# Hybrid attention layer on one core: other fillers in the head, and loads, a bias matmul and weight splits of the head in other places

## The chip, the cores and the metric

The kernel runs on one core of one Trainium2 chip. The time is device microseconds of one execution; three executions of the kernel before gave 317.7, 318.25 and 319.02 us, and 318.25 is their median.

## The reference, cut to what matters

One decoder layer for 512 tokens of width 1024. The head of the kernel, which the change touches, computes the modulation, the norm, and the first projection:

```
mod = silu(c) @ w_ada + b_ada
shift, scale, gate = jnp.split(mod, 3, axis=-1)
h = rms_norm(x, norm_gain) * (1 + scale[:, None, :]) + shift[:, None, :]
proj = h @ w_in
...
return x + gate[:, None, :] * out
```

`proj` splits into queries, keys, values and gates of two groups of heads (a sliding window of 128 with sinks; compressed, selected and window branches), whose outputs are gated, put together, multiplied by `w_out` and added to x. The relative bias of the heads comes from a table of 32 buckets.

## The kernel before, in words

x is held transposed, as eight tiles `xT[k]` of 128 features by 512 tokens. One block of the code, under `in_order`, fixes the order of every engine's instructions to that in which they are written; it holds all of the head and the first projection (about the first 54 us). What comes after is written through generators, and a scheduler places it on the engines.

**Norm.** ScalarE (ACT) squares each `xT[k]` as it lands, VectorE (DVE) adds the squares of four tiles into one accumulator (`sq` for tiles 0 to 3, `sacc` for 4 to 7; tile 7 in two halves), and TensorE (PE) sums each accumulator over the partitions into `pr` (L330). DVE makes the reciprocal root `rx` of the four blocks of tokens in some nine small steps; PE transposes it into `rbp`, a row of factors on all partitions (L352); ACT keeps a copy, `rb` (L364). `scaled(k)` multiplies `xT[k]` by it (DVE, L270).

**Modulation.** Each tile k needs a shift and a scale per feature, in `AB[:, k]`. For k = 0 and 1 PE computes them: `mod_pe(k)` multiplies silu(c) in `scz` by eight column blocks of w_ada in `ada[k]` (L230), ACT copies the result to `macc` (L233), `mod_col(k)` sums it over the partitions on PE (L250), and `mod_ab(k)` writes AB on DVE (L255, L256). For k = 2 to 7 DVE does it alone: `mod_rows(k)` is two long multiply-and-sum instructions (L222) over `ada[k]` and `scrow`, the row silu(c) on all partitions. scrow is made from the row c that a DMA broadcasts: ACT computes `throw` (L373), DVE multiplies (L376).

**First projection.** For each k, `h_high` makes hh[k] and hf[k] on ACT (L276; L363, L365 for k = 0), `h_low` their difference hl[k] on DVE (L279); the weights `wst[k]` are split by ACT into swh (`weights_high`, L262) and by DVE into swl (`weights_low`, L265). `first_proj(k, n)` is eight matmuls (L286, L287): n = 0 takes hh and swh, n = 1 hh and swl, n = 2 hl and swh. Between n = 1 and n = 2 of tile k stands `new_tile(k + 1)`, that is h_high(k+1), mod_rows(k+2), h_low(k+1), scaled(k+2) and the split of weights k+2. In what follows FP is the start of first_proj(0, 0), and T the start of mod_rows(2).

**Loads.** All go through SyncE's queue (SP): eight tiles of x, `first` (c as a column, b_ada, the gain, the identity), `bl` (the table for the relative bias), then ada[k] and wst[k] by turns, the row c after wst[0], and `rest`. ada_ring and wst_ring hold four tiles each. ada[k] comes in two halves.

**Fillers.** `dummies(n)` are n matmuls of a zero tile of 512 columns (L312), whose results nobody reads. The table ND says how many stand at five places: 20 at the start, 4 after the first sums, 2 after the bias matmul and before mod_pe(0), 2 between the transposes and mod_col(0), 3 after it.

**Relative bias.** PE multiplies the two parts of `bl` (L343) into `pl`, ACT copies the result to `lsb` (L345) and spreads its last columns (L346), and two DMAs write it to `line_d`, from where the attention reads it at about 49 us.

Of the kernel before, what the change touches and what calls it, by code (L numbers as in the profile page):

```python
# [13 lines left out]
AF = mybir.ActivationFunctionType  # L14
OP = mybir.AluOpType
# [4 lines left out]
S, D, HD, NB = 512, 1024, 64, 4  # L20
# [5 lines left out]
LINE = 640  # L26
# [3 lines left out]
WAIT_L, WAIT_M = 4, (0, 8)  # L30
PER_A, PER_B = 3.6, (3.5, 1.6, 7)
NEAR = 256
ND = (20, 2, 2, 3, 4)
NR = 4
LW = 4
PE_MODS = 2
# [45 lines left out]
def hybrid_layer_kernel(ctx, tc, A, out):  # L82
# [117 lines left out]
    def load_ada(k):  # L200
        t = ada_ring[:, k % NR]
        if k < PE_MODS:
            ada[k] = t.rearrange("p (a b c) -> p a b c", a=8, b=2)
            for e in range(2):
                SP.dma_start(ada[k][:, 4 * e:4 * e + 4], A["w_ada_cols"][k][:, 4 * e:4 * e + 4])
        else:
            ada[k] = t.rearrange("p (a b) -> p a b", a=2)
            for e in range(2):
                SP.dma_start(ada[k][:, e], A["w_ada_rows"][k - PE_MODS][:, e])

    def load_wst(k):
        wst[k] = wst_ring[:, k % NR]
        SP.dma_start(wst[k], A["w_qkv_a"][k])
# [8 lines left out]
            DVE.tensor_tensor_reduce(out=ada[k][:, e], in0=ada[k][:, e], in1=scrow, scale=factor, scalar=start,  # L222
                                     op0=OP.mult, op1=OP.add, accum_out=AB[:, k, 1 - e:2 - e])

    def mod_pe(k):

        pm = ps_pj.tile([128, 512], F32, name="pj")[:, 0:256]
        for j in range(8):
            c = j % 4
            PE.matmul(pm[32 * c:32 * c + 32, :], scz[:, j, :], ada[k][:, j].rearrange("p a b -> p (a b)"),  # L230
                      start=j < 4, stop=j >= 4, skip_group_check=True)
        macc[k] = stp.tile([128, 2, 128], F32, name="macc0", bufs=2)
        ACT.activation(macc[k].rearrange("p a b -> p (a b)"), pm, AF.Copy)  # L233
# [18 lines left out]
    def mod_ab(k):  # L252

        pc = pcs.pop(k)
        DVE.tensor_tensor(AB[:, k, 1:2], pc[:, 0:1], prm[:, k:k + 1], op=OP.add)  # L255
        DVE.scalar_tensor_tensor(AB[:, k, 0:1], pc[:, 1:2], prm1[:, k:k + 1], prm[:, 24 + k:25 + k],  # L256
                                 op0=OP.add, op1=OP.mult)

    def weights_high(k):

        ws[k] = (stp.tile([128, 768], F32R, name="swh", bufs=3), stp.tile([128, 768], F32R, name="swl", bufs=3))
        ACT.activation(ws[k][0], wst[k], AF.Copy)  # L262

    def weights_low(k):
        DVE.tensor_tensor(ws[k][1], wst[k], ws[k][0].bitcast(F32), op=OP.subtract)  # L265
# [24 lines left out]
    with in_order(tc) as begun:  # L290
        zero = con.tile([128, 512], BF16, name="zero")
        DVE.memset(zero, 0.0)
        DVE.memset(ada_ring[:, 0, 0:1], 0.0)
        DVE.memset(wst_ring[:, 0, 0:1], 0.0)
        POOL.memset(lsb[0:8, 0:LINE - NEAR], BIG)
        for k in range(8):
            SP.dma_start(xT[k], A["xT"][k])
        SP.dma_start(first, A["first"])
        SP.dma_start(bl, A["bias"])
        for k in range(NR):  # L300
            load_ada(k)
            load_wst(k)
            if k == 0:
                src = A["c"]
                SP.dma_start(scrow, bass.AP(tensor=src.tensor, offset=src.offset, ap=[[0, 128], [1, D]]))
        SP.dma_start(rest, A["rest"])
        DVE.memset(scz, 0.0)


        def dummies(n):  # L310
            for _ in range(n):
                PE.matmul(pj_kv[0].rearrange("p a b -> p (a b)"), zero[:, 0:128], zero, start=True, stop=True)  # L312

        dummies(ND[0])

        halves = [slice(0, 256), slice(256, 512)]
        pr = ps_pj.tile([128, 512], F32, name="pj")
        pl = pj_q[1][0:40, 0:NEAR]
        th = con.tile([128, 8], F32, name="th")
        for k in range(8):  # L320
            sq = stp.tile([128, S], F32, name="sacc") if k == 4 else T2(F32, "sq")
            if k % 4 == 0:
                sacc = sq
            for c in (halves if k == 7 else [slice(0, S)]):
                ACT.activation(sq[:, c], xT[k][:, c], AF.Square)
                if k % 4:
                    DVE.tensor_tensor(sacc[:, c], sacc[:, c], sq[:, c], op=OP.add)
            if k % 4 == 3:
                for tb in range(NB):
                    PE.matmul(pr[:, tb:tb + 1], sacc[:, tb * 128:(tb + 1) * 128], ones, start=k == 3 and tb == 0,  # L330
                              stop=k == 7 and tb == NB - 1, skip_group_check=True)
            if k == 3:
                dummies(ND[4])
        ACT.activation(th, cT, AF.Tanh, scale=0.5)
        DVE.scalar_tensor_tensor(sc_col, th, 1.0, cT, op0=OP.add, op1=OP.mult)
        DVE.tensor_scalar(scz[:, :, 0], sc_col, 0.5, None, op0=OP.mult)
        sx = con.tile([128, NB], F32, name="sx")
        DVE.tensor_scalar(sx, pr[:, 0:NB], 1.0 / D, EPS, op0=OP.mult, op1=OP.add)
        rx = rsqrt(sx, NB)
        DVE.tensor_scalar(prm1, prm[:, 8:16], 1.0, None, op0=OP.add)  # L340
        DVE.tensor_tensor(prmg[:, 0:8], prm1, prm[:, 24:32], op=OP.mult)
        DVE.tensor_scalar(prmg[:, 8:16], prm[:, 24:32], 0.5, None, op0=OP.mult)
        PE.matmul(pl, bl[:, NEAR:NEAR + 40], bl[:, 0:NEAR], start=True, stop=True)  # L343
        dummies(ND[1])
        ACT.copy(lsb[0:40, LINE - NEAR:LINE], pl)  # L345
        ACT.copy(lsb[32:40, 0:LINE - NEAR], lsb[32:40, LINE - NEAR:LINE - NEAR + 1].to_broadcast([8, LINE - NEAR]))  # L346
        for a in range(2):
            SP.dma_start(line_d[a], lsb[32 * a:32 * a + 8, :])
        mod_pe(0)
        rbp = ps_pj.tile([128, 512], F32, name="pj")  # L350
        for tb in range(NB):
            PE.transpose(rbp[:, tb * 128:(tb + 1) * 128], rx[:, tb:tb + 1].to_broadcast([128, 128]), ident)  # L352
        dummies(ND[2])
        mod_col(0)
        dummies(ND[3])
        weights_high(0)
        scaled(0, rbp, halves[:1])
        mod_ab(0)
        scaled(0, rbp, halves[1:])
        rb = stp.tile([128, S], F32, name="rb")  # L360
        hf[0] = T2(F32, "hf")
        for c in halves:
            ACT.activation(hh[0][:, c], y[0][:, c], AF.Identity, bias=AB[:, 0, 1:2], scale=AB[:, 0, 0:1])  # L363
        ACT.activation(rb, rbp, AF.Copy)  # L364
        ACT.activation(hf[0], y[0], AF.Identity, bias=AB[:, 0, 1:2], scale=AB[:, 0, 0:1])  # L365
        weights_low(0)
        scaled(1, rb)
        h_low(0)
        weights_high(1)
        weights_low(1)  # L370
        throw = T2(F32, "throw"), T2(F32, "throw")
        for e in range(2):
            ACT.activation(throw[e], scrow[:, 512 * e:512 * e + 512], AF.Tanh, scale=0.5)  # L373
        for e in range(2):
            v = scrow[:, 512 * e:512 * e + 512]
            DVE.scalar_tensor_tensor(v, throw[e], 1.0, v, op0=OP.add, op1=OP.mult)  # L376

        def new_tile(k):

            h_high(k, halves if k < 4 else (slice(0, S),))  # L380
            if k < 7:
                mod_rows(k + 1)
            h_low(k)
            if k < 7:
                scaled(k + 1, rb)
                weights_high(k + 1)
                weights_low(k + 1)

        for k in range(8):
            if k + NR < 8:  # L390
                load_ada(k + NR)
                load_wst(k + NR)
            elif k == LW:
                for _ in range(5):
                    load_next()
            for n in range(3):
                first_proj(k, n)
                if k == 0 and n == 0:
                    mod_pe(1)
                if k < 7 and n == 1:  # L400
                    if k == 0:
                        mod_col(1)
                        mod_ab(1)
                    new_tile(k + 1)
                if k >= 6 and n == 1:
                    split_to("kv_cmp", 2 * (k - 6) + 1, 0)
        DVE.tensor_tensor(kg[:, 0], qga, kga, op=OP.mult)
        DVE.tensor_tensor(kg[:, 1], qgb, kgs, op=OP.mult)
        DVE.tensor_tensor(kg[:, 2], qgb, kgw, op=OP.mult)
        DVE.tensor_tensor(kg[:, 3], qgb, kgc, op=OP.mult)  # L410
        DVE.tensor_scalar(kg[:, 0:3], kg[:, 0:3], -(HD ** -0.5), None, op0=OP.mult)
        DVE.tensor_scalar(kg[:, 3], kg[:, 3], HD ** -0.5, None, op0=OP.mult)
        DVE.tensor_scalar(nsink, sinks, -1.0, None, op0=OP.mult)
# [678 lines left out]
```

## Time and profile before

| what | value |
|---|---|
| median of three executions | 318.25 us |
| the profiled execution | 317.4 us, of which the profile's span is 315.6 us |
| PE / DVE / ACT busy | 307.2 / 237.4 / 195.7 us |
| first_proj(0, 0) begins (FP) | 17.63 us |
| mod_rows(2) begins on DVE (T) | 22.46 us |
| the first projection ends, the next matmuls begin | 54.34 us |

The profiled execution lies 0.85 us below the median of the three others. All clock times below are microseconds from the start of its span. A row of the timeline has the start, the length, the engine with the line of the code, the operation with what it writes and reads, and the count of instructions merged into it.

### The profile page before, as it was taken

What the parts mean: (1) busy time and instruction counts of PE and PEld (TensorE: products, weight loads), DVE (VectorE), ACT (ScalarE), POOL (GpSimd) and SP (SyncE); (2) the same over time, 40 slices, a digit from 0 to 9 for tenths busy, and PEclk for the clock granted to TensorE, in tenths of its full rate; (3) what the DMA queues carried; (4) which work ended last, traced back from release to release, by engine and by line L of the source; (5) the groups of instructions that cost most, each with busy time, mean ns of one, the idle gap of its engine ahead of it and who ended that gap; (6) DMA issues with size and microseconds to landing.
All of it is one profiled execution on the core that took longest, in us unless ns stands there. A gap on an engine that the chain in (4) does not pass through costs nothing.

```text
span 315.6 us, 5830 instructions
## 1 busy us (share of the span) xinstructions
PE 307.2 (97%) x2122; PEld 252.3 (80%) x2122; DVE 237.4 (75%) x658; ACT 195.7 (62%) x472; POOL 3.9 (1%) x21
## 2 busy tenths in 40 slices
PE   8899999999999999999999999999999999999995
PEld 3468888788988999889883888878788878788885
DVE  3589999999967558898997998988686777544221
ACT  5476557668967675676927767778785777513000
POOL 0000000000000000000000000000000000000000
PEclk9799999999999999999999999999999999999999
DMA  7999967900291908170553004222320210242201
GB/s 241 380 412 411 405 233 197 340 11 0 62 345 35 293 5 251 51 266 2 175 177 145 5 2 133 69 66 70 134 69 0 69 66 3 74 159 98 104 33 69
DMA packets 28232, 44.65 MB, mean 141 GB/s; under 512 B 1787, under 2 KB 19612, under 8 KB 28204
## 3 DMA queue, kind: packets, MB, share of 16 engines
q1 hardware_dynamic: 27052, 42.18, 39.4%
q10 hardware_dynamic: 1152, 2.10, 2.0%
q8 instruction: 17, 0.28, 0.4%
q14 instruction: 11, 0.09, 0.1%
HBM read 42.13 MB, written 2.14 MB: 140 GB/s over the span
## 4 chain that ended last, share of the span: by engine, by line
PE 79%; DVE 10%; ACT 6%; DMA 2%; issue 1%; SPq 1%; POOL 0%; ACTq 0%; DVEq 0%; POOLq 0%
PE pj L469 29%; PE pj L459 9%; PE sq L286 8%; PE po L930 7%; PE s L855 7%; PE pt L913 4%; PE skv L287 4%; PE pt L903 3%; PE s L588 3%; DVE qs L520 2%; DMA xTp<-in_xT 2%; DVE kTb L538 1%; PE po L936 1%; DVE raw L690 1%; DVE wl L174 1%
## 5 line engine op out<-in xcount | busy, mean ns | idle before, releaser
L173 ACT ACTIVATE wh<-raw 128x512 fp32r<-128x512 f32 (+1 forms) x52 | 31.2, 637 | 13.5 <-PE pj L469 13.4
L174 DVE TENSOR_TENSOR wl<-raw,wh 128x512 fp32r<-128x512 f32 (+1 forms) x52 | 34.8, 689 | 5.2 <-ACT wh L173 3.5
L459 PE MATMUL pj<-wh,hh 128*128 128x256 f32 (+1 forms) x128 | 37.0, 289 | 0.0
L459 PE MATMUL pj<-wl,hh 128*128 128x256 f32 (+1 forms) x128 | 36.7, 287 | 0.1
L459 PE MATMUL pj<-wh,hl 128*128 128x256 f32 (+1 forms) x128 | 36.6, 286 | 0.0
L867 ACT ACTIVATE pp<-pp,nm 128x256 f32<-128x256 f32 (+2 forms) x48 | 29.3, 614 | 6.6 <-DVE nm L860 6.4
L469 PE MATMUL pj<-hh,wh 128*128 128x512 f32 x80 | 32.1, 402 | 0.0
L469 PE MATMUL pj<-hh,wl 128*128 128x512 f32 x80 | 32.0, 400 | 0.0
L469 PE MATMUL pj<-hl,wh 128*128 128x512 f32 x80 | 31.8, 398 | 0.0
L860 DVE CUSTOM_DVE_ANT_0 pp<-s,bias 128x256 f32<-128x256 f32 (+2 forms) x48 | 25.5, 551 | 3.6 <-PE s L855 3.5
L469 PE MATMUL pj<-yl,wh 128*128 128x512 f32 (+1 forms) x72 | 26.6, 372 | 0.0
L469 PE MATMUL pj<-yh,wh 128*128 128x512 f32 (+1 forms) x72 | 26.6, 371 | 0.0
L469 PE MATMUL pj<-yh,wl 128*128 128x512 f32 (+1 forms) x72 | 26.4, 369 | 0.0
L1018 DVE SCALAR_TENSOR_TENSOR fin<-pj,gate,xr 128x512 f32<-128x512 f32 (+1 forms) x9 | 6.2, 691 | 25.1 <-PE pj L469 25.1
L459 PEld LDWEIGHTS pj<-wl,hh 128*128 128x128 f32 x128 | 24.1, 188 | 0.4 <-DVE wl L174 0.3
L459 PEld LDWEIGHTS pj<-wh,hh 128*128 128x128 f32 x128 | 24.1, 188 | 0.3 <-issue 0.2
L459 PEld LDWEIGHTS pj<-wh,hl 128*128 128x128 f32 x128 | 24.1, 188 | 0.2 <-issue 0.2
L855 PE MATMUL s<-kTb,qs 128*128 128x256 f32 (+2 forms) x96 | 23.5, 356 | 0.0
L888 DVE TENSOR_SCALAR pp<-pp,rr,grev 128x256 f32<-128x256 f32 (+2 forms) x48 | 21.1, 475 | 0.7
L914 ACT COPY ptT<-pt 128x384 f32<-128x384 f32 (+1 forms) x32 | 15.7, 531 | 7.0 <-PE pt L913 6.7
L904 ACT COPY ptT<-pt 128x512 f32<-128x512 f32 (+1 forms) x28 | 15.5, 552 | 5.2 <-PE pt L903 4.9
L469 PEld LDWEIGHTS pj<-hh,wh 128*128 128x128 f32 x80 | 15.0, 188 | 3.9 <-issue 1.2
(232 smaller groups left out, 709.2 us busy)
## 6 DMA issues: line engine op xcount, KB each, us to landing
ada_ring<-in_w_ada_rows SPq DMA_DIRECT2D x12, 512.0 KB, 9.3
raw<-in_w_cmp SPq DMA_DIRECT2D x8, 512.0 KB, 6.4
raw<-in_w_gate SPq DMA_DIRECT2D x8, 512.0 KB, 5.0
raw<-in_w_o SPq DMA_DIRECT2D x8, 512.0 KB, 3.8
wst_ring<-in_w_qkv_a SPq DMA_DIRECT2D x8, 384.0 KB, 9.3
xTp<-in_xT SPq DMA_DIRECT2D x8, 256.0 KB, 4.7
ada_ring<-in_w_ada_cols SPq DMA_DIRECT2D x4, 512.0 KB, 7.1
bias<-line_d SPq DMA_DIRECT2D x8, 256.0 KB, 3.4
```

What stands on the lines that cost most here:

```text
L173: ACT.activation(wh, src, AF.Copy)
L174: DVE.tensor_tensor(wl, src, wh.bitcast(F32), op=OP.subtract)
L286: PE.matmul(pj_q[tb], lt, w[:, 0:512], start=f, stop=l, skip_group_check=True)
L459: PE.matmul(bank[:, t * n:(t + 1) * n], h[:, tb * 128:(tb + 1) * 128], w[:, k % 2, :], start=k == 0 and m == 0, stop=k == 7 and m == 2)
L469: PE.matmul(bank, w, h[:, tok], start=k == 0 and m == 0, stop=k == 7 and m == 2)
L855: PE.matmul(ps, qs[h][:, 128 * i:128 * i + 128], k[:, hl_, lo:lo + w], start=hl_ == 0, stop=hl_ == 1)
L860: DVE.tensor_tensor_reduce(out=P[:, g, 0:w], in0=ps, in1=bt, scale=1.0, scalar=init, op0=OP.add, op1=OP.min, accum_out=nm[:, g:g + 1])
L867: ACT.activation(P[:, g, 0:e], P[:, g, 0:e], AF.Exp, bias=nm[:, g:g + 1], scale=-1.0, accum_out=dn[:, g:g + 1])
L888: DVE.tensor_scalar(v, v, rr[:, g:g + 1], gates[:, g, br:br + 1], op0=OP.mult, op1=OP.mult)
L904: ACT.copy(T[:, :, 0:nb, :], rev(pt[:, 0:2 * nb * 128].rearrange("p (g b q) -> p g b q", g=2, b=nb)))
L914: ACT.copy(T[:, 0:nb, :], rev(pt[:, 0:nb * 128].rearrange("p (b q) -> p b q", b=nb)))
L930: PE.matmul(o[64 * g:64 * g + 64, 128 * i:128 * i + 128], vb[:, 64 * g:64 * g + 64], sl["T"][g][:, b, :], start=first_of and b == 0, stop= ...
```

## The change

- The 20 fillers at the start become 11. In their place come fillers that read data as it arrives: 13 small float32 products of `xT[k]` with itself (0, 0, 2, 3, 2, 2, 3, 1 for k = 0 to 7), placed ahead of each square, and 1 and 2 that read the halves of the last square. The first sums move from after the square of tile 3 to after the fillers of tile 4; the 4 fillers behind them go.
- 3 zero fillers stand ahead of mod_pe(0), 2 in its middle, 1 after it, none between the transposes and mod_col(0), 3 behind the bias matmul.
- ada[0] comes in a half and two quarters. `bl` is loaded behind it and not ahead of it, the row c behind wst[1] and not behind wst[0].
- The bias matmul moves behind mod_col(0), into another bank; its first copy on ACT behind the halves of hh[0], the second one ahead of macc of tile 1.
- weights_high(1) and throw move behind mod_pe(1) on ACT, weights_low(1) and scrow behind mod_ab(1) on DVE.

DVE from scaled(1) (row with `rb`) and hl of tile 0 to mod_rows(2) (the `ISA` rows), before:

```order
L270 TENSOR_TENSOR xTp<-xTp,rb 128x512
L279 TENSOR_TENSOR hl_84<-hf,hh_76 128x512
L265 TENSOR_TENSOR swl<-wst_ring,swh 128x768
L376 SCALAR_TENSOR_TENSOR scrow<-throw,scrow 128x512 x2
L255 TENSOR_TENSOR AB<-pj,first 128x1
L256 SCALAR_TENSOR_TENSOR AB<-pj,prm_98,first 128x1
L222 ISA ada_ring,AB<-ada_ring,scrow,first 128x1024
```

The same stretch of DVE in the changed kernel:

```order
L272 TENSOR_TENSOR xTp<-xTp,rb 128x512
L281 TENSOR_TENSOR hl_84<-hf,hh_76 128x512
L257 TENSOR_TENSOR AB<-pj,first 128x1
L258 SCALAR_TENSOR_TENSOR AB<-pj,prm_98,first 128x1
L267 TENSOR_TENSOR swl<-wst_ring,swh 128x768
L415 SCALAR_TENSOR_TENSOR scrow<-throw,scrow 128x512 x2
L222 ISA ada_ring,AB<-ada_ring,scrow,first 128x1024
```

The split swl of tile 1 and both halves of scrow stood ahead of mod_ab(1) and stand behind it now.

PE from the second sums (`sacc`) to the first rows of the first projection, before; the fillers are the rows with `zero`, `pj<-ada_ring,scz` is mod_pe(0), `pj<-first,n_y` the transposes, `pj<-ones,macc` mod_col(0):

```order
L330 MATMUL pj<-ones,sacc 128x1 x4
L343 MATMUL sq_120<-raw 40x256
L312 LDWEIGHTS zero
L312 MATMUL skv_123<-zero 128x512
...
L230 MATMUL pj<-ada_ring,scz 32x256 x8
L352 MATMUL pj<-first,n_y 128x128 x4
...
L250 MATMUL pj<-ones,macc_248 128x1 x2
...
L286 MATMUL sq_119<-swh,hh_76 128x512
```

The same stretch of PE in the changed kernel, with the rows that come just ahead of it:

```order
L316 MATMUL skv_123<-xTp 128x128 x6
L316 MATMUL skv_123<-sq 128x128 x3
L327 MATMUL pj<-ones,sacc 128x1 x4
...
L232 MATMUL pj<-ada_ring,scz 32x256 x4
...
L232 MATMUL pj<-ada_ring,scz 32x256 x4
...
L360 MATMUL pj<-first,n_y 128x128 x4
L252 MATMUL pj<-ones,macc_250 128x1 x2
L362 MATMUL sq_122<-raw 40x256
...
L288 MATMUL sq_119<-swh,hh_76 128x512
```

Nine float32 fillers now stand ahead of the second sums, mod_pe(0) is cut in the middle, and the bias matmul (`sq<-raw`) went from ahead of mod_pe(0) to behind mod_col(0).

The rest of the program, which the scheduler places, has the same instructions; on PE their order is another one from the 34th matmul of kv_cmp (35 stood in a row), to the second group of weighted values (`po`), that is from about 62 to 114 us of the trace, and the same after that.

```diff
-ND = (20, 2, 2, 3, 4)
+ND = (11, (0, 0, 2, 3, 2, 2, 3, 1), (1, 2), 3, 2, 1, 3)
...
-            for e in range(2):
-                SP.dma_start(ada[k][:, 4 * e:4 * e + 4], A["w_ada_cols"][k][:, 4 * e:4 * e + 4])
+            for e, n in ((0, 4), (4, 2), (6, 2)) if k == 0 else ((0, 4), (4, 4)):
+                SP.dma_start(ada[k][:, e:e + n], A["w_ada_cols"][k][:, e:e + n])
...
+            if j == 4:
+                between()
...
-        SP.dma_start(bl, A["bias"])
         for k in range(NR):
             load_ada(k)
+            if k == 0:
+                SP.dma_start(bl, A["bias"])
             load_wst(k)
-            if k == 0:
+            if k == 1:
                 src = A["c"]
                 SP.dma_start(scrow, bass.AP(tensor=src.tensor, offset=src.offset, ap=[[0, 128], [1, D]]))
...
+        def fillers(n, over=None):
             for _ in range(n):
-                PE.matmul(pj_kv[0].rearrange("p a b -> p (a b)"), zero[:, 0:128], zero, start=True, stop=True)
+                l, m = (zero[:, 0:128], zero) if over is None else (over[:, 0:128], over[:, 128:256])
+                PE.matmul(pj_kv[0].rearrange("p a b -> p (a b)")[:, 0:m.shape[1]], l, m, start=True, stop=True)
...
-        pl = pj_q[1][0:40, 0:NEAR]
+        pl = pj_q[3][0:40, 0:NEAR]
...
+            fillers(ND[1][k], xT[k])
+            if k == 4:
+                sums(sacc_a, True, False)
...
+                if k == 7:
+                    fillers(ND[2][n], sq[:, c])
...
-        PE.matmul(pl, bl[:, NEAR:NEAR + 40], bl[:, 0:NEAR], start=True, stop=True)
-        dummies(ND[1])
-        ACT.copy(lsb[0:40, LINE - NEAR:LINE], pl)
-        ACT.copy(lsb[32:40, 0:LINE - NEAR], lsb[32:40, LINE - NEAR:LINE - NEAR + 1].to_broadcast([8, LINE - NEAR]))
-        for a in range(2):
-            SP.dma_start(line_d[a], lsb[32 * a:32 * a + 8, :])
-        mod_pe(0)
+        fillers(ND[3])
+        mod_pe(0, lambda: fillers(ND[4]))
+        fillers(ND[5])
...
-        dummies(ND[2])
         mod_col(0)
-        dummies(ND[3])
+        PE.matmul(pl, bl[:, NEAR:NEAR + 40], bl[:, 0:NEAR], start=True, stop=True)
+        fillers(ND[6])
...
+        ACT.copy(lsb[0:40, LINE - NEAR:LINE], pl)
         ACT.activation(rb, rbp, AF.Copy)
...
-        weights_high(1)
-        weights_low(1)
...
                 if k == 0 and n == 0:
                     mod_pe(1)
+                    weights_high(1)
+                    for e in range(2):
+                        ACT.activation(throw[e], scrow[:, 512 * e:512 * e + 512], AF.Tanh, scale=0.5)
                 if k < 7 and n == 1:
                     if k == 0:
                         mod_col(1)
                         mod_ab(1)
+                        weights_low(1)
+                        for e in range(2):
+                            v = scrow[:, 512 * e:512 * e + 512]
+                            DVE.scalar_tensor_tensor(v, throw[e], 1.0, v, op0=OP.add, op1=OP.mult)
                     new_tile(k + 1)
```

More of the change, by code (lines that the diff above doesn't have):

```diff
@@ L223, in mod_rows, with mod_pe @@
                                      op0=OP.mult, op1=OP.add, accum_out=AB[:, k, 1 - e:2 - e])
-    def mod_pe(k):
+    def mod_pe(k, between=lambda: None):
         pm = ps_pj.tile([128, 512], F32, name="pj")[:, 0:256]
@@ L307, in hybrid_layer_kernel, with sums @@
         DVE.memset(scz, 0.0)
-        def dummies(n):
+        def fillers(n, over=None):
             for _ in range(n):
-                PE.matmul(pj_kv[0].rearrange("p a b -> p (a b)"), zero[:, 0:128], zero, start=True, stop=True)
-        dummies(ND[0])
+                l, m = (zero[:, 0:128], zero) if over is None else (over[:, 0:128], over[:, 128:256])
+                PE.matmul(pj_kv[0].rearrange("p a b -> p (a b)")[:, 0:m.shape[1]], l, m, start=True, stop=True)
+        fillers(ND[0])
         halves = [slice(0, 256), slice(256, 512)]
         pr = ps_pj.tile([128, 512], F32, name="pj")
-        pl = pj_q[1][0:40, 0:NEAR]
+        pl = pj_q[3][0:40, 0:NEAR]
         th = con.tile([128, 8], F32, name="th")
+        def sums(acc, f, l):
+            for tb in range(NB):
+                PE.matmul(pr[:, tb:tb + 1], acc[:, tb * 128:(tb + 1) * 128], ones, start=f and tb == 0,
+                          stop=l and tb == NB - 1, skip_group_check=True)
         for k in range(8):
@@ L323, in hybrid_layer_kernel @@
                 sacc = sq
-            for c in (halves if k == 7 else [slice(0, S)]):
+            fillers(ND[1][k], xT[k])
+            if k == 4:
+                sums(sacc_a, True, False)
+            for n, c in enumerate(halves if k == 7 else [slice(0, S)]):
                 ACT.activation(sq[:, c], xT[k][:, c], AF.Square)
@@ L327, in hybrid_layer_kernel @@
                     DVE.tensor_tensor(sacc[:, c], sacc[:, c], sq[:, c], op=OP.add)
[L328 to L331, printed above, removed]
+                if k == 7:
+                    fillers(ND[2][n], sq[:, c])
             if k == 3:
-                dummies(ND[4])
+                sacc_a = sacc
+        sums(sacc, False, True)
         ACT.activation(th, cT, AF.Tanh, scale=0.5)
@@ L368, in hybrid_layer_kernel @@
         h_low(0)
-        weights_high(1)
-        weights_low(1)
+        ACT.copy(lsb[32:40, 0:LINE - NEAR], lsb[32:40, LINE - NEAR:LINE - NEAR + 1].to_broadcast([8, LINE - NEAR]))
+        for a in range(2):
+            SP.dma_start(line_d[a], lsb[32 * a:32 * a + 8, :])
         throw = T2(F32, "throw"), T2(F32, "throw")
[L372 to L376, printed above, removed]
         def new_tile(k):
```

## The prediction

> **What bounds the kernel now.** I read the page's totals, then the granted clock by half microseconds, the timeline of PE, DVE and ACT in the head, the waits, and last the busy time by stage.
>
> ```profile
> span 315.6 us, 5830 instructions
> PE 307.2 (97%) x2122; PEld 252.3 (80%) x2122; DVE 237.4 (75%) x658; ACT 195.7 (62%) x472; POOL 3.9 (1%) x21
> ```
>
> PE is hardly ever idle, so the end moves with PE; the question is what PE waits for in the stage behind the head. First the head, PE:
>
> ```profile
> 8.76 1.02 PE L312 MATMUL skv<-zero 128*128 128x512 bf16 x4
> 10.60 1.05 PE L330 MATMUL pj<-ones,sacc 128*128 128x1 f32 x8 [0.81 <-DVE sacc L327]
> 11.58 0.62 PE L343 MATMUL sq<-raw 33*40 33x256 f32 x2
> 12.14 1.04 PE L312 MATMUL skv<-zero 128*128 128x512 bf16 x2
> 13.11 1.93 PE L230 MATMUL pj<-ada_ring,scz 128*32 128x256 f32 x16
> 14.97 0.89 PE L352 MATMUL pj<-first,n_y 128*128 128x128 f32 x4
> 16.12 0.50 PE L250 MATMUL pj<-ones,macc 128*128 128x1 f32 x4
> 17.63 0.50 PE L286 MATMUL sq<-swh,hh 128*128 128x512 f32 x1 [0.34 <-ACT hh L363]
> 19.22 1.07 PE L230 MATMUL pj<-ada_ring,scz 128*32 128x256 f32 x16
> 21.72 0.50 PE L250 MATMUL pj<-ones,macc 128*128 128x1 f32 x4
> ...
> 12.00:12.50 0.50, 0.50 (x2) 0.13 (x2) 0.40 (x4) 0.26 (x1) 0.00 (x0) 0.57 1.06 428
> 15.00:15.50 0.50, 0.50 (x7) 0.50 (x4) 0.00 (x0) 0.38 (x1) 0.00 (x0) 0.52 1.00 410
> ```
>
> From 10.60 to 16.6 PE works without a gap, and what it does there is serial: sums, bias matmul, fillers, mod_pe(0), transposes, fillers, mod_col(0). mod_pe(0) takes 1.93 us where the same work for tile 1 takes 1.07: the granted clock (the seventh figure) falls to half at about 12.1 and comes back at about 15.5. So the head has some 2 us to win. Now DVE behind it:
>
> ```profile
> 20.03 0.96 DVE L265 TENSOR_TENSOR swl<-wst_ring,swh 128x768 fp32r<-128x768 f32 x1
> 20.90 1.29 DVE L376 SCALAR_TENSOR_TENSOR scrow<-throw,scrow 128x512 f32<-128x512 f32 x2
> 22.26 0.16 DVE L255 TENSOR_TENSOR AB<-pj,first 128x1 f32<-128x1 f32 x1
> 22.46 1.27 DVE L222 CUSTOM_DVE_ANT_0 ada_ring<-ada_ring,scrow,first 128x1024 f32<-128x1024 f32 x1
> 27.00 1.28 DVE L222 CUSTOM_DVE_ANT_0 ada_ring<-ada_ring,scrow,first 128x1024 f32<-128x1024 f32 x1
> ...
> 28.00:30.00 2.00, 2.00 (x13) 1.80 (x12) 2.00 (x5) 1.14 (x2) 0.00 (x0) 1.00 1.02 400
> 38.00:40.00 2.00, 2.00 (x12) 1.53 (x11) 2.00 (x5) 0.05 (x1) 0.00 (x0) 1.00 1.02 398
> ...
> ACT hh L276 <- DVE xTp L270: 11.2, 6, 2.3
> PEld sq L286 <- DVE hl L279: 1.1, 4, 0.3
> ```
>
> DVE is busy for 2.00 of 2.00 us (third figure), a tile costs it 4.54 us (22.46 to 27.00), ACT waits 11.2 us for `scaled`, and PE for hl. PE needs less for a tile: 12 pairs of matmuls at 0.35 us, 4.2 us (a pair is 22.87 to 23.22 below). So from T = 22.46 on the first projection is bound by DVE, and its end by T. PE is 0.34 us per tile faster and has caught up with DVE by the fourth tile, with whatever lead it starts.
>
> ```profile
> 22.87 0.39 PE L286 MATMUL sq<-swh,hl 128*128 128x512 f32 x1
> 23.22 0.39 PE L286 MATMUL sq<-swh,hl 128*128 128x512 f32 x1
> ```
>
> **The change part by part.**
>
> *Fillers ahead of the second sums.* Of the 20 at the start 9 go, and the 4 behind the first sums. Nine float32 fillers come between the first sums (whose last load ends where the fillers begin, 8.76) and the second ones. A float32 product runs as two passes (L330: 4 written, x8 in the trace). The nearest rows for a pass of 128 columns are the sums, with one column but the same weight load, and four transposes of this size later; the rows by line give the length of one (ns, least, median and most):
>
> ```profile
> 104.45 0.66 PE L903 MATMUL pt<-first,pa 128*128 128x128 f32 x4
> L903 PE MATMUL pt<-first,pa x56: 272/273/330, 77.3 to 153.4; 128*128 128x128 f32 x56
> L330 PE MATMUL pj<-ones,sacc x8: 250/250/271, 10.6 to 11.4; 128*128 128x1 f32 x8
> L312 PE MATMUL skv<-zero x31: 376/379/634, 1.2 to 16.9; 128*128 128x512 bf16 x31
> ```
>
> A sum is (1.05 - 0.25)/7 = 0.11 us from start to start, a transpose (0.66 - 0.27)/3 = 0.13. So 0.22 to 0.26 us a filler; I take 0.24, nearer the transposes, since columns stream too: 9 x 0.24 = 2.2 us, from 8.76 to 10.9. The sums were free to begin at 10.60, so they come 0.3 us later (0.1 to 0.5).
>
> *The chain from the sums to FP, at full clock.* Sums 0.98 (10.60 to 11.58): 11.9. Three fillers at 0.21 (four in 1.02 us at 8.76, less the length of one, 0.38, over three): 12.5. Half of mod_pe(0), 0.43, two fillers 0.43, the other half 0.43: 13.8. One filler, 14.0, transposes 4 x 0.11: 14.5. The transposes need the norm's steps on DVE, which take from the sums' end to 13.43:
>
> ```profile
> 11.69 0.16 DVE L338 TENSOR_SCALAR sx<-pj 128x4 f32<-128x4 f32 x1 [0.52 <-PE pj L330]
> 13.27 0.16 DVE L108 SCALAR_TENSOR_TENSOR n_y<-n_t,n_y 128x4 f32<-128x4 f32 x1
> 15.11 0.38 ACT L233 ACTIVATE macc<-pj 128x256 f32<-128x256 f32 x1 [1.96 <-PE pj L230]
> ```
>
> 1.74 us behind sums that end at 11.95: 13.7, in cover. mod_col(0) waits for macc, 0.45 us behind mod_pe(0)'s last end (15.04 to 15.49, now 14.0): 14.5. From there to FP as before, 16.12 to 17.63, 1.51 us: **FP = 16.0**, against 17.63, 1.6 us earlier. The bias matmul and three fillers behind mod_col(0) lie in that stretch: 0.36 + 0.50 + 0.65 us, just 1.51, covered to within 0.1.
>
> *ada[0] in three pieces.* The second half is issued at 6.43 and lands 6.5 us later, 12.9:
>
> ```profile
> 5.77 0.99 SPq L205 DMA_DIRECT2D ada_ring<-in_w_ada_cols  x2
> ada_ring<-in_w_ada_cols SPq DMA_DIRECT2D x1, 512.0 KB, 6.5
> scrow<-in_c SPq DMA_DIRECT2D x1, 512.0 KB, 7.2
> ```
>
> The chain above asks for it at 13.4. Without `bl` in front it lands earlier (38 KB; nothing to half a microsecond). Cost and gain 0; a third issue on SP is 0.3 us, and the queue runs some 6 us ahead of landing.
>
> *c behind wst[1].* Before it landed at 7.86 + 7.2 = 15.1; ada[1] and wst[1], 1.4 MB, now go first, 3.4 us at the 410 GB/s of the windows: 18.5. ACT wants it at about 19.8, behind mod_pe(1) and the split of weights. 0.
>
> *Copies of the bias on ACT.* 0.36 us now stand ahead of `rb` and hf[0], 0.51 ahead of macc of tile 1:
>
> ```profile
> 12.24 0.36 ACT L345 COPY raw<-sq 40x256 f32<-40x256 f32 x1 [2.12 <-PE sq L343]
> 12.64 0.51 ACT L346 COPY raw<-raw 8x384 f32<-8x384 f32 x1
> 17.98 0.57 ACT L364 ACTIVATE rb<-pj 128x512 f32<-128x512 f32 x1
> ```
>
> ACT ends hh[0] about FP + 0.4, so rb at FP + 1.3, macc free at FP + 2.5; mod_pe(1), which reuses rbp's bank, begins at FP + 1.6 (17.63 to 19.22) and ends at FP + 2.6. Covered, by 0.1 to 0.3 us; if the cover goes, it costs as much.
>
> *weights_low(1) and scrow behind mod_ab(1).* This is the term that decides. Before, DVE did both while PE was at mod_pe(1) and first_proj(0, 1), and came to mod_ab(1) at 22.26, just when mod_col(1) ended (21.72 + 0.50). Now DVE sits idle until mod_col(1), and both follow: T = FP + 4.63 (17.63 to 22.26, PE's own work) + 0.20 (22.26 to 22.46) + 0.87 (20.03 to 20.90) + 1.29 = FP + 6.99. With FP = 16.0, **T = 23.0, against 22.46: 0.5 us later.** No FP after 15.5 gains anything, and the chain reaches 15.7 at best, with no delay of the sums.
>
> *Order of the scheduled part.* The same instructions stand in another order from 62 to 114 us. PE's whole idle time between 40 and 150 bounds a gain:
>
> ```profile
> sum 110.00, PE 107.95 PEld 96.80 DVE 92.20 ACT 77.58 POOL 3.29; mean PE 4.91 PEld 4.40 DVE 4.19 ACT 3.53 POOL 0.15
> ```
>
> 2.05 us; a loss has no bound in a row, I put 1 us by the same measure. I take 0.
>
> *Sum.* 1.6 us won at FP, 2.2 us of DVE work put behind mod_ab(1): +0.5 us on the profiled 317.4, that is 317.9. That execution lies 0.85 us below the median; on the median, 318.25 + 0.5 = 318.8.
>
> **The clock, a rival.** The half clock above lasted 3.4 us (12.1 to 15.5), though the longest gap of PE ahead of it was 0.81 us. [...]
>
> **Rivals.**
> 1. *The clock stays at half in the head.* For it: the 9 fillers taken from the start and pauses for each x tile leave PE emptier up to 8.7 us; against it, 9 fillers more stand just ahead of the sums. mod_pe(0) then takes 0.9 us more, six zero fillers 0.2 each, but part of it overlaps: FP about 17.4, T = 24.4, 1.9 us after before: 320.1.
> 2. *The other side: the head's gain reaches the end.* PE begins the projection 1.6 us earlier and keeps it. It decides at FP: if DVE had 2.2 us of slack between mod_ab(1) and hl of the fourth tile, the end would follow PE: 318.25 - 1.6 = 316.6. For it: PE is 97% busy and hl makes it wait 1.1 us in all. Against: DVE's 2.00 of 2.00, and ACT's 11.2 us.
> 3. *The scheduled part decides:* a microsecond either way, 317.8 or 319.8.
>
> **How the numbers follow.** Forecast (DVE gives back the head's gain) 0.55, half clock 0.24, the gain kept 0.13, the scheduled part 0.08. Executions of before differ by 1.3 us (0.4%), so 0.5%, 1.6 us, is about what a measurement tells. Faster by more: most of rival 2 and a little of 3, 0.13. Slower by more: two thirds of rival 1 and the edge of the others, 0.22. The same: 0.65. The range goes from rival 2's 316.7 to a little over rival 1's, 320.4.
>
> **What would show it.** Right: FP near 16.0; the swl and scrow rows behind mod_ab(1) and an idle DVE of some 2 us ahead of it; T at 23; waits of PE for hl larger than 1.1 us; the projection's end at about 54.8. mod_pe(0) near 1.5 us with its two fillers at full clock. Wrong: T before 22, or a stage with DVE under 2.00; then the order of DVE was not the limit.

## The result, and the profile of the changed kernel

The changed kernel took 320.69 us (median of 8, 320.27 to 321.73), the kernel before beside it 318.34 us: ratio 1.0073, interval 1.0047 to 1.0099. A second series (e11 below) gave 321.06 against 318.0 us, 1.0081 [1.0055, 1.0108]. It is slower by 2.4 to 3.1 us; the forecast was 318.8, and the range ended at 320.4.

The page's totals, then the timeline of PE in the head. This first profile, of 321.73 us, is of the longest of the eight executions; that of e11 took 321.20, near its median, and every row from the squares of x on stands 0.5 us earlier there, so the comparison with the forecast goes by e11's rows.

```profile
span 319.4 us, 5891 instructions
PE 307.9 (96%) x2142; PEld 254.1 (80%) x2143; DVE 237.8 (74%) x658; ACT 196.6 (62%) x472; POOL 4.0 (1%) x21
```

PE in the head of e11, the same kernel:

```profile
9.41 1.58 PE L316 MATMUL skv<-xTp 128*128 128x128 f32 x12
10.83 0.83 PE L316 MATMUL skv<-sq 128*128 128x128 f32 x6
11.50 0.95 PE L327 MATMUL pj<-ones,sacc 128*128 128x1 f32 x8
13.05 0.64 PE L232 MATMUL pj<-ada_ring,scz 128*32 128x256 f32 x8
14.15 0.64 PE L232 MATMUL pj<-ada_ring,scz 128*32 128x256 f32 x8
15.39 0.51 PE L252 MATMUL pj<-ones,macc 128*128 128x1 f32 x4
16.91 0.52 PE L288 MATMUL sq<-swh,hh 128*128 128x512 f32 x1
```

The last row is FP: 16.91, 0.7 us ahead of before's 17.63. Each half of mod_pe(0) takes 0.64 us, and the mean granted clock of both profiles is 1.000, where before's is 0.995: the half clock of the head is gone. Then DVE of the first profile, from mod_ab(1) to T:

```profile
22.10 0.16 DVE L257 TENSOR_TENSOR AB<-pj,first 128x1 f32<-128x1 f32 x1 [2.04 <-PE pj L252]
22.30 0.95 DVE L267 TENSOR_TENSOR swl<-wst_ring,swh 128x768 fp32r<-128x768 f32 x1
23.16 1.29 DVE L415 SCALAR_TENSOR_TENSOR scrow<-throw,scrow 128x512 f32<-128x512 f32 x2
24.49 1.28 DVE L222 CUSTOM_DVE_ANT_0 ada_ring<-ada_ring,scrow,first 128x1024 f32<-128x1024 f32 x1
```

DVE stands idle for 2.04 us ahead of mod_ab(1), and does swl and scrow behind it. T = 24.49 (23.98 in e11), against 22.46. Behind T the windows show DVE as the bound, as before, and among the waits those of PE's weight load for hl have grown from 1.1 to 3.6 us:

```profile
30.00:32.00 2.00, 2.00 (x13) 1.66 (x11) 2.00 (x5) 1.16 (x2) 0.00 (x0) 1.00 1.03 405
PEld sq L288 <- DVE hl L281: 3.6, 7, 1.6
```

Where the 3.8 us between the profiles of e11 (321.20) and of before (317.40) went, from four marks of each trace and the time outside the span:

| stretch | before | e11 | difference |
|---|---|---|---|
| start of the span to FP | 17.63 | 16.91 | -0.72 |
| FP to T | 4.83 | 7.07 | +2.24 |
| T to the end of the first projection | 31.72 | 31.74 | 0.0 |
| from there to the first matmul of the output projection | 201.74 | 203.48 | +1.74 |
| from there to the end of the span | 59.69 | 59.66 | 0.0 |
| outside the span | 1.8 | 2.3 | +0.5 |

So the head lost 1.5 us, the attention (56 to 259 us, whose instructions the change does not touch) 1.7 us, and 0.5 us lies outside the span, in all 14 executions of the changed kernel (2.2 to 2.4 us).

### The profile page after: what moved, and what is told of

It is laid out like the page before. It is cut to its first block, busy times and chain, and to the rows that moved or that the text cites. A ratio compares the mean times of both kernels' runs of the same rounds, so it can differ in the third digit from the quotient of the medians.

```text
span 319.4 us, 5891 instructions
## 1 busy us (share of the span) xinstructions
PE 307.9 (96%) x2142; PEld 254.1 (80%) x2143; DVE 237.8 (74%) x658; ACT 196.6 (62%) x472; POOL 4.0 (1%) x21
## 4 chain that ended last, share of the span: by engine, by line
PE 79%; DVE 13%; ACT 4%; issue 2%; DMA 2%; SPq 0%; DVEq 0%; ACTq 0%
PE pj L481 30%; PE po L942 8%; PE sq L288 8%; PE s L867 7%; PE pj L471 5%; PE pt L925 4%; PE skv L289 4%; PE pt L915 3%; PE s L600 2%; DVE qs L532 2%; DVE wl L174 2%; DMA xTp<-in_xT 2%; DVE pa L872 1%; PE skv L316 1%; PE po L948 1%
```

## The experiments

Three things were taken apart: the place of swl, scrow, swh and throw of tile 1 ("late", as in the change, or "early", ahead of the first projection, as before), the new head's fillers and loads, and the rows, that is the order of the scheduled part on PE, DVE, ACT and SP. The rows were fixed by tying each engine's instructions behind the head into the sequence that the named kernel has (no new waits between engines). Buffers were left to the pools, which deal them during the build, and could not be fixed with this.

| kernel | head | DVE's place | rows | median us | ratio [95%] | FP | T | T to projection's end | projection's end to output projection |
|---|---|---|---|---|---|---|---|---|---|
| before | old | early | old | 317.9 to 318.3 | 1 | 17.63 | 22.46 | 31.72 | 201.74 |
| changed, e11 | new | late | new | 321.06 | 1.0081 [1.0055, 1.0108] | 16.91 | 23.98 | 31.74 | 203.48 |
| e1 | new | late | old | 319.64 | 1.0044 [1.0025, 1.0064] | 17.21 | 24.27 | 31.78 | 202.54 |
| e2 | old | early | new | 318.85 | 1.0022 [0.9995, 1.0048] | 18.69 | 23.51 | 31.73 | 202.38 |
| e3 | old | late | old | 321.64 | 1.0107 [1.0072, 1.0141] | 20.00 | 27.05 | 31.77 | 202.47 |
| e4 | new | early | old | 317.51 | 0.998 [0.9959, 1.0000] | 17.11 | 22.72 | 31.73 | 201.74 |
| e5 | new, c early | early | old | 317.42 | 0.9983 [0.9959, 1.0007] | 17.06 | 22.66 | 31.73 | 201.70 |
| e6 | as e5, scrow first | early | old | 318.44 | 1.0014 [0.9996, 1.0031] | 16.27 | 21.78 | 32.27 | 202.46 |
| e7 | as e6 | early | new | 317.77 | 0.9992 [0.9973, 1.0012] | 16.24 | 21.75 | 31.80 | 202.20 |
| e8 | as e5, no fillers on x | early | old | 319.85 | 1.0056 [1.0035, 1.0077] | 18.55 | 24.16 | 31.74 | 201.72 |
| e9 | as e5, second copy later | early | old | 317.20 | 0.997 [0.9952, 0.9988] | 16.72 | 21.65 | 32.04 | 201.72 |
| e10 | as e9, fewer fillers | early | old | 317.96 | 0.9989 [0.9968, 1.0011] | 17.26 | 22.19 | 32.04 | 201.75 |

FP, T and the stretches are from one profile each, us; the projection's end is taken at the start of the first matmul behind it (54.18 in before; the last matmul of the projection ends at 54.34). FP moves by half a microsecond and more between executions, with the landing of x (17.44 in the first profile of the changed kernel, whose last square of x begins and all later rows stand 0.5 us behind e11's, with 16.91) and, in the old head, with the half clock: the profiles of e2 and e3 have it for 6.83 us (11.10 to 17.92, 11.79 to 18.61; mean clock 0.989), that of before for 3.41 (0.995). The stretches behind T repeat to 0.1 us: 31.78 and 203.44 in the first profile of the changed kernel, 31.74 and 203.48 in e11.

**e1, the changed kernel with the old rows, and e2, the old kernel with the new rows.** The edit in both is the tying alone:

```
+    for row in LAID:            # LAID: PE, DVE, ACT, SP rows of the other kernel
+        for p, i in zip(row, row[1:]):
+            tc.add_manual_dep(i, p.name, info, reason="in_order")
```

> The changed kernel's head; behind the first projection every engine's order is held to that of the kernel before. In the two profiles 2.1 us of the loss stand at the end of the first projection and 1.7 us come behind it. If the other order of the scheduled part costs those 1.7 us, this kernel takes 320.7 - 1.7 = 319.0 us (1.002 of before). If the order costs nothing and the 1.7 us come from something else, 320.7 us (1.007).

> The head of the kernel before; behind the first projection every engine's order is held to that of the changed kernel. If the order costs 1.7 us: 318.3 + 1.7 = 320.0 us (1.005), with the first projection ending at 54.2 us as before. If it costs nothing: 318.3 us.

e1 took 319.64, 1.05 us under the changed kernel's 320.69 in another series (the intervals of the ratios overlap), and its attention is 0.9 us shorter. In e2 the new rows made it 0.64 us longer, and by the ratio the time 0.7 us longer, with an interval that takes in no change. So the rows cost, but 0.6 to 0.9 us and not the 1.7 of the profiles; e1 still spends 0.8 us more than before in the attention, in before's own rows.

**e3, the old head with DVE's late place, and e4, the new head with the early one.** e3 moves these lines of the kernel before, e4 moves them back in the changed one; both have the old rows.

```
-        weights_high(1)
-        weights_low(1)
-        ACT.activation(throw[e], ...)                                     # for e in 0, 1
-        DVE.scalar_tensor_tensor(v, throw[e], 1.0, v, ...)                # for e in 0, 1
...
                     mod_pe(1)
+                    weights_high(1)
+                    ACT.activation(throw[e], ...)
...
                         mod_ab(1)
+                        weights_low(1)
+                        DVE.scalar_tensor_tensor(v, throw[e], 1.0, v, ...)
```

> The kernel before, with one part of the change: the split of weights 1, throw and scrow stand behind mod_pe(1) on ACT and behind mod_ab(1) on DVE, as in the changed kernel. The scheduled part keeps its order of before. If DVE's order sets T: FP 17.6 as before, T = FP + 7.0 = 24.6 against 22.46, the first projection ends 2.1 us later, 318.3 + 2.1 = 320.4 us (1.0066). If PE's start FP sets the end: FP and the time as before, 318.3 us.

> The changed kernel with that part undone: the split of weights 1, throw and scrow stand ahead of the projection again, on ACT and DVE; all else of the head is the changed one, the order behind it that of before. If DVE's order sets T: T falls from FP + 7.0 to FP + 4.8, held up a little by c's row, which lands at about 18.5, and by macc of tile 1 behind throw on ACT, so T about 22.0 to 22.5 and 317.8 to 318.4 us (0.998 to 1.000), some 1 to 2 us under the run with the new head and the old order. If not: no different from that run.

The place on DVE is decided: late, T - FP is 7.05 to 7.07 in three kernels; early it is 4.8 (before, e2) and 5.6 (e4). With the early place the new head is no slower than before. e3 and e4 fit the forecast's mechanism. But e3, like e1, also has 0.75 us more in the attention, and e4 has exactly before's 201.74. e3's FP was expected at 17.6 and came at 20.00, with the longer half clock of its profile (6.83 us) and a last square of x that begins at 9.91 (9.30 in before). Its median lies 3.7 us over before's, more than 2.2 us at T and 0.75 in the attention make. It has six executions: at a mean clock of 0.995 they took 320.58, 320.73 and 321.16 us, at 0.989 322.15 and 322.74, and at these clocks before's medians beside them are 317.8 and 319.6, which leaves 2.8 to 3.0 us; the sixth, at 0.994, took 322.12.

**Buffers: e6 and e7.** Laid over before's trace, e1 and e3 fall behind in small steps at the same matmuls: 0.19 at 119, 0.1 at 122, 0.13 at 163, 0.33 at 171 us of before's span; the changed kernel has the last two at the same matmuls, and one of 0.27 near 121. The largest, first in the kernel before, then in the changed one (ACT, then PE):

```profile
169.09 0.62 ACT L173 ACTIVATE wh<-raw 128x512 fp32r<-128x512 f32 x1
171.80 1.05 PE L646 MATMUL pj<-qs,kTc 128*32 128x512 f32 x2 [0.38 <-DVE qs L520]
```

```profile
173.52 0.63 ACT L173 ACTIVATE wh<-raw 128x512 fp32r<-128x512 f32 x1 [0.82 <-PE pj L481]
175.66 1.05 PE L658 MATMUL pj<-qs,kTc 128*32 128x512 f32 x2 [0.70 <-DVE qs L532]
```

The same copy of weights waits 0.82 us for a matmul in the changed kernel: the trace does not name the buffer, but the wait fits another buffer of the ring of `wh`, whose last reader is later. Counted in the traces, 38 of the 104 copies and differences of weights behind the head wait for another number of semaphores in e1, e3 and e6 than in before, 2 or 3 in e4 and e5, 14 in e7. Moving throw ahead of the weights, with an early T, deals the buffers as in e1; without the tying they come out nearly as before. That gives two more kernels, e6 tied to the old rows and e7 not tied, which comes out with the new ones:

```
+        ACT.activation(throw[e], ...); DVE.scalar_tensor_tensor(v, ...)   # e6, e7
         weights_high(1)
         weights_low(1)
-        ACT.activation(throw[e], ...); DVE.scalar_tensor_tensor(v, ...)
```

> As e5, but throw and scrow stand ahead of the split of tile 1's weights. Behind the head the rows are those of the kernel before, but the tiles of weights and of probabilities lie in other buffers of their rings: nearly as in e1. T = FP + 4.8 as in e5 by either theory. Theory (the buffers cost 0.8 us): from the end of the first projection to the output projection 202.5 us as in e1 and e3, and not 201.7 as in the kernel before and e4, with the same steps at the last matmuls on qs and at pj<-qs,kTc; 0.8 us more than e5, 317.6 us. Rival (those 0.8 us belong to a late T, in e1 and e3, and not to the buffers): 201.7 and the time of e5, 316.8 us.

> As e6, but behind the head the rows are those of the changed kernel; its buffers lie nearly as those of the kernel before. Theory (rows and buffers cost separately, rows 0.6 to 0.9 us): 202.3 to 202.6 us from the first projection's end to the output projection, the loss at 62 to 114 us and no step later; 317.4 to 317.7 us. Rival (only buffers cost): 201.7, and 316.8 us.

e6's attention took 202.46 us with T at 21.78, so a late T is not what costs, and the two rows are there again, with the difference of the weights on DVE, which passes the wait on to qs and so to PE:

```profile
170.26 0.63 ACT L179 ACTIVATE wh<-raw 128x512 fp32r<-128x512 f32 x1 [0.82 <-PE pj L488]
170.93 0.69 DVE L180 TENSOR_TENSOR wl<-raw,wh 128x512 fp32r<-128x512 f32 x1 [0.37 <-ACT wh L179]
172.40 1.04 PE L665 MATMUL pj<-qs,kTc 128*32 128x512 f32 x2 [0.72 <-DVE qs L539]
```

The times agree less well than the stretches: e6 took 318.44 where 317.6 was expected; e5, on which that stood, had itself come 0.6 us over its 316.8, and T - FP is 5.51 in e6 and e7, not 4.8. Half a microsecond of e6's time was lost between T and the projection's end (32.27), of which the trace gives 0.4 to one wait of DVE ahead of a swl with nothing shown. e7's new rows cost 0.46 us without the buffers' steps; its 317.77 is 0.35 above e5. The loss lies before 120 us. PE's busy time from 53.5 to 120 us in before, e6 and e7 (sum of the window; busy time of each engine):

```profile
sum 66.50, PE 65.43 PEld 58.00 DVE 52.95 ACT 49.41 POOL 3.10; mean PE 65.43 PEld 58.00 DVE 52.95 ACT 49.41 POOL 3.10
```

```profile
sum 66.50, PE 65.44 PEld 57.90 DVE 52.61 ACT 49.67 POOL 2.65; mean PE 65.44 PEld 57.90 DVE 52.61 ACT 49.67 POOL 2.65
```

```profile
sum 66.50, PE 64.91 PEld 57.42 DVE 52.36 ACT 48.95 POOL 3.32; mean PE 64.91 PEld 57.42 DVE 52.36 ACT 48.95 POOL 3.32
```

With the old rows PE is idle for 1.07 and 1.06 us, with the new ones for 1.59. Rows 0.5 to 0.65 and buffers 0.7 to 0.8 make 1.2 to 1.45 of the changed kernel's 1.74; it has a third set of buffers, and the rest was not taken apart. The traces show where some 0.4 us of it lies: the first weighted values (`po<-ptT,va`) begin 59.38 us behind the projection's end in before (at 113.56), 60.47 in e11 (116.19), and only 60.11 and 60.03 in e2 and e7 (115.35, 113.58).

**e5 and e9: what held up mod_ab(1) in e4.** e5 puts c's row back behind wst[0] (`if k == 0:` for `if k == 1:`); e9 also moves the second copy of the bias:

```
-        ACT.copy(lsb[32:40, 0:LINE - NEAR], ...)      # and its two DMAs to line_d
...
                     mod_pe(1)
+                    ACT.copy(lsb[32:40, 0:LINE - NEAR], ...)
```

> The changed head with the split of tile 1's weights and scrow back ahead of the first projection, as in e4, and c's row back behind wst[0]; behind the head the rows of the kernel before. Theory: in e4 the third step on ACT (macc of tile 1) stood behind throw, which waited for c, so mod_ab(1) came 5.4 us behind FP and not 4.7; with c early T = FP + 4.8, so 0.7 us before e4's: T = 22.0, and 316.8 us, ratio 0.996. Rival: c's place is worth nothing, time as e4's (317.5, 0.998).

> As e5, but the second copy of the bias on ACT (0.51 us, 8x384) and its two DMAs stand behind mod_pe(1), so behind macc of tile 1. Theory: in e4 and e5 the two copies (0.35 and 0.51 us) hold up ACT ahead of swh, throw and macc of tile 1, so that mod_col(1) waits 0.39 us for macc and mod_ab(1) comes 5.4 us behind FP; without the second copy T = FP + 5.1, 0.5 us before e5's, and 316.9 us. Rival (DVE's swl and scrow hold up mod_ab(1) whatever ACT does): T = FP + 5.6, 317.4 us.

My theory of e5 fell: c early changed nothing (317.42, T - FP 5.6 again). In its trace ACT never waits for c; it is simply full (from 16.41 to 21.66 without a wait), and behind the second copy swh comes late for swl on DVE, and macc for PE. ACT, DVE and PE of e5, then of e9:

```profile
18.98 0.51 ACT L384 COPY raw<-raw 8x384 f32<-8x384 f32 x1
19.51 0.84 ACT L270 ACTIVATE swh<-wst_ring 128x768 fp32r<-128x768 f32 x1
20.39 0.96 DVE L273 TENSOR_TENSOR swl<-wst_ring,swh 128x768 fp32r<-128x768 f32 x1 [0.71 <-ACT swh L270]
21.27 1.29 DVE L394 SCALAR_TENSOR_TENSOR scrow<-throw,scrow 128x512 f32<-128x512 f32 x2
22.47 0.15 DVE L263 TENSOR_TENSOR AB<-pj,first 128x1 f32<-128x1 f32 x1
21.72 0.61 PE L258 MATMUL pj<-ones,macc 128*128 128x1 f32 x4 [0.39 <-ACT macc L241]
```

```profile
18.51 0.83 ACT L270 ACTIVATE swh<-wst_ring 128x768 fp32r<-128x768 f32 x1
19.38 0.96 DVE L273 TENSOR_TENSOR swl<-wst_ring,swh 128x768 fp32r<-128x768 f32 x1
20.25 1.29 DVE L391 SCALAR_TENSOR_TENSOR scrow<-throw,scrow 128x512 f32<-128x512 f32 x2
21.46 0.15 DVE L263 TENSOR_TENSOR AB<-pj,first 128x1 f32<-128x1 f32 x1
20.84 0.50 PE L258 MATMUL pj<-ones,macc 128*128 128x1 f32 x4
```

In e5 swl waits 0.71 us for swh, and scrow and mod_ab(1) follow it without a gap. PE's wait for macc, which both theories went by, is not what ended last: mod_col(1) is done at 22.33, ahead of mod_ab(1) at 22.47. With the copy behind macc both waits are gone and T - FP is 4.93 (5.1 was expected). Of the 0.67 us won at T, 0.31 are lost again by the projection's end (32.04 behind T, not 31.73): the last hl waits 1.09 us for hf there, and 0.78 in e5. e9 is faster than before by 0.3%, 0.4 to 1.5 us by its interval, and has the lowest median of the twelve.

**e8 and e10: what the fillers on x do.** e8 is e5 without the 16 fillers on x and its squares, e10 is e9 without the last seven of them (the expectations miscount them as 18 and 6):

```
-ND = (11, (0, 0, 2, 3, 2, 2, 3, 1), (1, 2), 3, 2, 1, 3)
+ND = (11, (0, 0, 0, 0, 0, 0, 0, 0), (0, 0), 3, 2, 1, 3)      # e8
+ND = (11, (0, 0, 2, 3, 2, 2, 0, 0), (0, 0), 3, 2, 1, 3)      # e10
```

> As e5 without the 18 fillers that read x's tiles and squares; the 11 at the start and those behind the second sums stay. Theory (the fillers stand in front of the second sums for 0.5 us, and the clock doesn't need them): second sums 1.3 us behind the last square of x and not 1.8, FP 0.5 us earlier than in e5, 316.3 us, ratio 0.994, full clock. Rival 1 (they hold the clock): half clock over mod_pe(0) as in the kernel before, which takes 1.9 us and more, FP 0.5 to 1.5 us later than in e5, 317.3 to 318.3 us. Rival 2 (the landing of x alone sets the sums): as e5.

> As e9 without the 6 last fillers (those that read tile 6, tile 7 and the squares of tile 7); 2, 3, 2 and 2 on tiles 2 to 5 stay. Theory: the second sums begin 1.3 us behind the last square and not 1.6 to 1.9 (0.4 us earlier), and the clock stays full, since the gap of PE ahead of the sums is under 1.5 us: T 0.4 us before e9's, 316.5 us, ratio 0.996. Rival (each stretch without fillers ahead of the sums brings the half clock, as in e8): half clock over mod_pe(0), 318 to 319.5 us.

Both my theories were half right: the sums did follow sooner, and the half clock came back, so the rivals hold. ACT's last squares (four merged) and PE's second sums, in e11 and in e8:

```profile
8.34 2.04 ACT L338 ACTIVATE sq<-xTp 128x512 f32<-128x512 f32 x4
11.50 0.95 PE L327 MATMUL pj<-ones,sacc 128*128 128x1 f32 x8
```

```profile
7.80 2.10 ACT L344 ACTIVATE sq<-xTp 128x512 f32<-128x512 f32 x4
10.54 1.86 PE L333 MATMUL pj<-ones,sacc 128*128 128x1 f32 x8 [1.58 <-DVE sacc L346]
13.63 1.08 PE L238 MATMUL pj<-ada_ring,scz 128*32 128x256 f32 x8
10.00:10.50 0.50, 0.00 (x0) 0.00 (x0) 0.44 (x2) 0.01 (x1) 0.00 (x0) 0.50 0.90 246
```

The sums begin 1.12 us behind the end of the squares with the fillers (10.38 to 11.50), 0.64 without (9.90 to 10.54): the fillers delay them by 0.5 us. Without them the same sums take 1.86 us and not 0.95, half of mod_pe(0) 1.08 and not 0.64, and the window row gives a granted clock of 0.50; the profile has it at half from 9.19 to 16.02. FP is 18.55. In e10, where PE's gap ahead of the sums was 1.18 us, half clock lasted from 10.85 to 14.26, so the 1.5 us of my theory was a limit that no run shows; FP came 0.5 us behind e9's; 9 of its 12 executions show a mean clock of 0.995 or less. So the fillers pay: they cost 0.5 us ahead of the sums, and without them the time rose by 2.4 us (e8 against e5). In the two profiles the difference is 1.5 us, all of it ahead of FP (18.55 against 17.06). Two of e8's executions show a mean clock of 0.999 and still took 319.79 and 319.91 us; no trace shows these two, so it is not shown that the half clock makes the whole of the 2.4 us.

**e11, the changed kernel again.**

> The changed kernel as it is, on the same chip as e9 and e10, for its times beside them. If the parts add up, it takes e9's time plus 1.3 us (T = FP + 7.05 and not 5.1 to 5.6, with the second copy in place), 0.8 us for other buffers and 0.6 us for the new rows: 319.6 us; its first result was 320.7 us, with 2.3 us outside the span where the kernel before has 1.8.

It took 321.06, 3.86 us over e9 on the same chip, where 2.4 us was expected. In the profiles (4.25 us): FP 0.2, T - FP 2.1 (I had 1.3 for it), behind T 1.4, and 0.5 outside the span, which I had named but not put into the sum.

## Why the prediction was wrong

The mechanism held, its cost on DVE was right to 0.1 us, and the sum failed by terms beside it. Against the profile that it started from (317.4 us, forecast 317.9), e11's 321.2 is 3.3 us too much:

- **T = FP + 6.99: right.** 7.05 to 7.07, and e3 against before and e1 against e4 show that the late place on DVE makes it. (T itself was 23.98 and not 23.0, and the projection's end 55.7 and not 54.8, by the next term.) The projection ends 31.72 to 31.80 us behind T in nine of the twelve kernels; rival 2, that the head's gain reaches the end, is refuted for the late place.
- **FP = 16.0: too early by 0.9 us.** The step that failed first is the start of the second sums, 10.9: it was 11.50. The squares ended 0.35 us later than before (10.38 against 10.03), which no term allowed for, and the fillers delayed the sums by 0.5 and not 0.3 us. The second is mod_pe(0) with its two fillers: from 13.05 to 14.79, 1.74 us, where I had 1.5 (12.5 to 14.0, its last end). From one half to the next it is 1.10 us (13.05 to 14.15) and not 0.86: the eight matmuls of a half take 0.64 us from first start to last end, and I took the half of a row in which sixteen follow each other, 0.43. Another 0.1 us lies ahead of mod_col(0).
- **The scheduled part, taken as 0 with at most 1 us of loss: wrong, +1.7 us, the largest of the errors.** Without it the measured 320.69 would be 319.0, inside the range; without FP's 0.9 us it would be 319.8. This was rival 3, to which I gave 0.08 and a microsecond. I looked at the rows only, and bounded the loss by PE's idle time. e2 and e7 price the rows at 0.5 to 0.65 us; another 0.7 to 0.8 us comes from buffers, which e1, e3 and e6 show and no comparison of rows does; the last 0.3 to 0.5 us stays open.
- **Time outside the span, +0.5 us.** Not foreseen. e1 has 2.0 and all the other kernels 1.8 us there, e7 with the same rows and e3 with the same place on DVE among them. What makes it stays open.
- **The 0.85 us added for the median was not due.** It brought the forecast nearer to the result for a wrong reason: before's executions spread with their mean clock, that is, by an estimate from the profiles, with how long half clock lasts (3.41 us and a mean of 0.995 in before's, 6.83 us and 0.989 in e2's and e3's), and the changed kernel shows none in the head. Of 23 executions of before beside e9 to e11, 16 show a mean clock of 0.994 to 0.998 and 317.07 to 318.36 us, 7 show 0.989 and 318.89 to 319.89; e9's 12 show 0.998 to 1.000 and 316.72 to 317.95.
- **Rival 1, half clock, 320.1: near the time, wrong in its cause.** The clock was 0.998 to 1.000 in every execution of the changed kernel. But it named the right danger: e8 and e10 lose to it.
- **Copies of the bias covered: right in the change** (mod_ab(1) at FP + 4.7), since macc stands ahead of swh and throw there; with these early the second copy is on the path, through swh and swl: 0.67 us of T, 0.36 us by the projection's end (e5 against e9).
- **c's row and ada[0] in pieces: 0**, as e4 against e5 shows for c; the pieces of ada[0] were not tried alone.

## What to carry to other kernels

Ahead of an engine that is the bound, compare what it must do behind the last input with what it can do while it waits: 2.2 us of work moved behind mod_ab(1) cost 2.2 us, whatever the head won. A change in one part of a kernel that a build schedules as a whole can re-deal rows and ring buffers elsewhere; look for both, and if the trace of the changed kernel drifts at places far from the edit, tie the old order down and compare. A range that takes such a drift as zero is too narrow; here it was 1.7 us of 320.

## What the runs showed of the hardware

- The half clock in the head lasted 3.41 us or twice that: 12.07 to 15.49 in before, 10.85 to 14.26 in e10 (3.41 us each), 9.19 to 16.02 in e8, 11.10 to 17.92 in e2 and 11.79 to 18.61 in e3 (6.83). In a span of 316 us, 3.41 us of it make a mean clock of 0.995, 6.83 us one of 0.989; before's profile has 0.995 and those of e2 and e3 0.989, while e10's 0.993 and e8's 0.988 lie a little under what these stretches make. Five of e8's executions show a mean clock of 0.984, which by the same sum would be three such pieces, an estimate. The length of PE's gaps does not tell where half clock comes: the longest near by were 0.81 us in before, 1.18 in e10, and 1.90 and 1.58 in e8, and the first profile of the changed kernel kept a clock of 1.00 behind one of 1.76 us (5.08 to 6.84). What it goes by is not shown.
- Small float32 products that nobody reads kept the clock full through the landing of x: with all 16 of them the mean clock was 0.998 to 1.000 in 85 of 86 executions (the changed kernel, e1, e4 to e7 and e9), in 2 of 12 without them (e8) and in 3 of 12 with nine of them (e10), for 0.5 us of delay to the sums.
- The last square of x began between 8.71 (e6) and 10.23 us (the first profile of the changed kernel), with the same eight loads first in the queue. The cause of this spread was not tried.
